# Query/key projection and gate/up: the token halves in the innermost loop of the matmuls

## The chip, the core and the metric

The kernel runs on one core of a Trainium2 chip. The metric is the device time of one execution in microseconds. The engines have these names in all rows: PE is TensorE's matmul, PEld its weight load (it runs beside PE), DVE is VectorE, ACT ScalarE, POOL GpSimd, SP SyncE, which issues the DMAs. Each engine works off its own instructions in order and waits for the others through semaphores.

## What is computed

A trunk of two layers over 1024 tokens of 1024 features in float32. The first layer mixes tokens by differential attention (8 heads, two softmax maps each), the second by neighbourhood attention (16 heads on a 16 x 64 grid). Around them stand norms, residual sums, a gated FFN with 2816 hidden units, and a gated input per layer:

```python
def swiglu(h, w_gate, w_up, w_down):
    return (jax.nn.silu(h @ w_gate) * (h @ w_up)) @ w_down
...
    for i in range(DEPTH):
        hn = rmsnorm(h, norm_mix[i])
        ...
            mix = diff_attention(hn, da_w_qkv[j], da_w_o[j], ...)
        ...
            mix = neighborhood_attention(hn, na_w_qkv[j], na_b_qkv[j], na_rpb[j], na_w_o[j])
        h = h + mix
        h = h + swiglu(rmsnorm(h, norm_ffn[i]), ffn_w_gate[i], ffn_w_up[i], ffn_w_down[i])
        gate = jax.nn.sigmoid(rmsnorm(h, norm_ple[i]) @ ple_w_gate[i])
        h = h + gate * (p[i] @ ple_w_proj[i])
    return rmsnorm(h, norm_final)
```

## The kernel before

**Products.** Every float32 matrix is held as two float32r parts, high and low (`split`, L87: one engine copies the high part, VectorE subtracts it from the source to get the low part). A product is three matmuls, high x high, high x low, low x high (`PASSES`, L49: stationary part, moving part). Line L131 (`mm_feat`) makes products whose result has features on the partitions: a weight tile of 128 x 128 is stationary, and a token half of 512 columns is moving. It is used for the query and key projections of both attentions (`qk`, L143) and for gate and up of the FFN (`hidden`, L532). Line L139 (`mm_tok`) makes products with tokens on the partitions (the down projection and out_proj): its innermost loop already runs over two halves of the columns, into two accumulators. L209 makes the values, L495 and L139 the two parts of out_proj, L595 and L599 the gated input.

**Operands.** The normalised tokens lie transposed in `hnT[0]` (tokens 0 to 511, token tiles 0 to 3) and `hnT[1]` (512 to 1023, tiles 4 to 7), in a pool on the right side of SBUF. In the orders of instructions below they are called hnT_95 and hnT_96 (layer 0, attention), hnT_6900 and hnT_6901 (layer 0, FFN), hnT_17330 and hnT_17331 (layer 1, FFN). `weights` (L94) loads 512 KB on SP's queue into a stage tile, GpSimd copies the high part into a slab on the left side (L91), VectorE writes the low part (L92). The pool in which out_proj_first keeps its operands (L495) takes the place of hnT while hnT is closed.

**Norm.** `norm_t` (L117) takes token tile t: ScalarE squares and sums (L111), GpSimd makes the factor (L112, L113), VectorE scales (L114), PE transposes eight 128 x 128 blocks (L124) into two PSUM tiles, ScalarE copies their high part into hnT (L89) and VectorE the low part (L92). At the end of out_proj each tile is first added to its residual by VectorE (L518).

**FFN.** For each of 22 hidden blocks of 128, gate and then up get an accumulator of 1024 columns (two PSUM banks, three such accumulators in all), then Silu on ScalarE reads the whole gate accumulator and VectorE multiplies by the whole of up. After every second block the down projection adds two blocks into the residual (L550).

**Attention.** The projections' accumulators of 512 columns come from a pool of two ("d"; four during the first projection). ScalarE reads an accumulator out into the high part (L162 to L166), VectorE into the low part (L170, L173), GpSimd copies the key to the other half of the partitions (L185).

**Order.** The program is written tile by tile, and a list scheduler decides, per engine, in which order the instructions are issued; a matmul whose accumulator isn't free, or whose operands aren't ready, can be passed by others when that order is made, but not when the program runs.

Of the kernel before, what the change touches and what calls it, by code (L numbers as in the profile page):

```python
# [12 lines left out]
F32 = mybir.dt.float32  # L13
# [7 lines left out]
P = 128  # L21
# [20 lines left out]
MASKED = -1e30  # L42
RING = 5
EARLY = 5
# heads whose two maps are scored together, so that their 64-row products share the array
PAIRED = 4
EXP_LN_SET = 6
# the three products that carry a float32 product: (stationary part, moving part)
PASSES = ((0, 0), (0, 1), (1, 0))  # L49


class Trunk:
# [21 lines left out]
        self.hs = self.dram.tile([NT, P, D], F32, name="hs")  # L74
        self.hp = self.dram.tile([NT, P, D], F32, name="hp")

# [1 line left out]
    def open_hn(self):  # L78
        self.hnpool = self.tc.alloc_tile_pool(name=self.nc.get_next_instruction_name(), bufs=1, side="right",
                                              reuse_waits="tile")  # L80
# [44 lines left out]
            ks = slice(4 * q, 4 * q + 4)  # L125
            self.split((dst[:, 0, ks, c], dst[:, 1, ks, c]), tr, self.nc.scalar)

    def mm_feat(self, ps, w, half):
        for kt in range(KT):
            for n, (i, j) in enumerate(PASSES):  # L130
                self.nc.tensor.matmul(ps, w[:, i, kt * P:(kt + 1) * P], self.hnT[half][:, j, kt, :],  # L131
                                      start=kt == 0 and n == 0, stop=kt == KT - 1 and n == 2)

    def mm_tok(self, ps, lhs, rhs, nk):
        for k in range(nk):
# [3 lines left out]
                    self.nc.tensor.matmul(ps[:, c], lhs(i, k), rhs(j, k, c),  # L139
                                          start=k == 0 and n == 0, stop=k == nk - 1 and n == 2)  # L140

# [1 line left out]
    def qk(self, u, pools, bias=None, q_scale=1.0):  # L143
        nc = self.nc
        qkp, psd = pools["qk"], pools["d"]
        qs = qkp.tile([P, 2, S], F32R, tag=f"qs{u % 2}", name="qs")
        kh = qkp.tile([P, 2, S], F32R, tag=f"kh{u % 2}", name="kh")
        kl = qkp.tile([P, S], F32R, tag=f"kl{u % 2}", name="kl")
        top, bot = slice(0, 64), slice(64, 128)
        for which in range(2):  # L150
            w = self.weights(pools["wqk"][2 * u + which], self.slab, "slab")
            b = None if bias is None else bias[:, which * 8 + u:which * 8 + u + 1]
            for half in range(2):
                c = slice(half * HALF, (half + 1) * HALF)
                ps = psd.tile([P, HALF], F32, tag="d", name="d")
                self.mm_feat(ps, w, half)

                sc = q_scale if which == 0 else 1.0

                def hi(out, rows):  # L160
                    if b is None and sc == 1.0:
                        nc.scalar.copy(out=out, in_=ps[rows])  # L162
                    elif b is None:
                        nc.scalar.activation(out=out, in_=ps[rows], func=AF.Copy, scale=sc)
                    else:
                        nc.scalar.activation(out=out, in_=ps[rows], func=AF.Identity, bias=b[rows], scale=1.0)  # L166

                def lo(out, rows, h):
                    if b is None:
                        nc.vector.scalar_tensor_tensor(out=out, in0=ps[rows], scalar=sc, in1=h.bitcast(F32),  # L170
                                                       op0=ALU.mult, op1=ALU.subtract)
                    else:
                        nc.vector.scalar_tensor_tensor(out=out, in0=ps[rows], scalar=b[rows], in1=h.bitcast(F32),  # L173
                                                       op0=ALU.add, op1=ALU.subtract)

                if which == 0:
                    hi(qs[top, 0, c], top)
                    hi(qs[bot, 1, c], bot)
                    lo(qs[bot, 0, c], top, qs[top, 0, c])
                    lo(qs[top, 1, c], bot, qs[bot, 1, c])  # L180
                else:
                    hi(kh[top, 0, c], top)
                    hi(kh[bot, 1, c], bot)
                    for m, (to, src) in enumerate(((bot, top), (top, bot))):
                        nc.gpsimd.tensor_scalar(out=kh[to, m, c], in0=kh[src, m, c].bitcast(F32), scalar1=1.0,  # L185
                                                scalar2=0.0, op0=ALU.mult, op1=ALU.add)
                    lo(kl[top, c], top, kh[top, 0, c])
                    lo(kl[bot, c], bot, kh[bot, 1, c])
        return qs, kh, kl
# [21 lines left out]
                                          start=k == 0 and n == 0, stop=k == KT - 1 and n == 2)  # L211
            sink(t, ps)

# [1 line left out]
    def diff_attention(self, first):  # L215
        nc, tc, a = self.nc, self.tc, self.a
        with ExitStack() as st:
# [133 lines left out]
                    ops = project(h + 1)  # L351
            self.out_proj_first(0, a["da_wo"], psd)

# [1 line left out]
    def neighborhood_attention(self):  # L355
        nc, tc, a = self.nc, self.tc, self.a
        with ExitStack() as st:
# [103 lines left out]
                    ops = self.qk(u + 1, pools, bq)  # L461
            self.out_proj_first(1, a["na_wo"], psd)

# [1 line left out]
    def keep(self, layer, u, ot):  # L465
        if u == PAIRS - 1:
            self.last = ot
# [54 lines left out]
    def ffn(self, layer, h, ps):  # L522
        nc, tc, a = self.nc, self.tc, self.a
        starts = [0] + list(range(1, NHID - 2, 2))
        with ExitStack() as st:
            actp = st.enter_context(tc.tile_pool(name=f"act{layer}", bufs=1, reuse_waits="tile"))
            wdp = st.enter_context(tc.tile_pool(name=f"wd{layer}", bufs=1, reuse_waits="tile"))
            gp = st.enter_context(tc.tile_pool(name=f"gf{layer}", bufs=1, reuse_waits="tile"))
            g = self.gain(3 * layer + 2, gp)
            acts, wds = {}, {}  # L530

            def hidden(n):  # L532
                pss = []
                for which in range(2):
                    w = self.weights(a["gu"][layer, n, which], self.slab, "slab")
                    acc = ps.tile([P, S], F32, tag="mm", name="mm")
                    for half in range(2):
                        self.mm_feat(acc[:, half * HALF:(half + 1) * HALF], w, half)
                    pss.append(acc)
                sil = self.t4.tile([P, S], F32, tag="t4", name="sil")  # L540
                nc.scalar.activation(out=sil, in_=pss[0], func=AF.Silu)  # L541
                nc.vector.tensor_tensor(out=sil, in0=sil, in1=pss[1], op=ALU.mult)  # L542
                acts[n] = actp.tile([P, 2, S], F32R, tag=f"act{n % 4}", name="act")
                self.split((acts[n][:, 0], acts[n][:, 1]), sil, nc.scalar)
                wds[n] = self.weights(a["wd"][layer, n * P:(n + 1) * P], wdp, f"wd{n % 3}")

            def down(c0, step):
                for t in range(NT):
                    acc = ps.tile([P, D], F32, tag="mm", name="mm")
                    self.mm_tok(acc, lambda i, k: acts[c0 + k][:, i, t * P:(t + 1) * P],  # L550
                                lambda j, k, c: wds[c0 + k][:, j, c], step)
                    nc.vector.tensor_tensor(out=h[t], in0=h[t], in1=acc, op=ALU.add)  # L552
                    if c0 + step >= NHID:
                        self.norm_t(h[t], t, g)

            for n in range(NHID):
                hidden(n)
                if n in starts[1:]:
                    c0 = starts[starts.index(n) - 1]
                    down(c0, n - c0)  # L560
            down(starts[-1], NHID - starts[-1])
# [77 lines left out]
        self.close_hn()  # L639


# [1 line left out]
def _units(w, n, width):  # L643
    k = w.shape[0]
    return w.reshape(k // P, P, n, width).transpose(2, 1, 0, 3)
# [64 lines left out]
```

## Time and profile before

| | us |
|---|---|
| median of 3 runs | 3075.58 |
| lowest and highest run | 3072.76, 3077.97 |
| span of the profiled execution | 3072.8 |
| PE busy in it | 3025.0 |
| VectorE, ScalarE, GpSimd busy | 1524.7, 783.0, 625.2 |

The profiled execution is the lowest of the three runs: its time, 3072.76 us, is its span. The stages follow one another: the first norm and projections (to 60 us), the attention of layer 0 (to 743), its out_proj and norm (to 803), its FFN (to 1525), the gated input (to 1648), the same for layer 1. Matmuls are pipelined: the duration of one, from its start to the modelled end, is longer than the distance to the next, so the busy time of PE is no measure of how fast it works.

### The profile page before, as it was taken

What the parts mean: (1) busy time and instruction counts of PE and PEld (TensorE: products, weight loads), DVE (VectorE), ACT (ScalarE), POOL (GpSimd) and SP (SyncE); (2) the same over time, 40 slices, a digit from 0 to 9 for tenths busy, and PEclk for the clock granted to TensorE, in tenths of its full rate; (3) what the DMA queues carried; (4) which work ended last, traced back from release to release, by engine and by line L of the source; (5) the groups of instructions that cost most, each with busy time, mean ns of one, the idle gap of its engine ahead of it and who ended that gap; (6) DMA issues with size and microseconds to landing.
All of it is one profiled execution on the core that took longest, in us unless ns stands there. A gap on an engine that the chain in (4) does not pass through costs nothing.

```text
span 3072.8 us, 36422 instructions
## 1 busy us (share of the span) xinstructions
PE 3025.0 (98%) x14304; PEld 2410.6 (78%) x14304; DVE 1524.7 (50%) x2793; ACT 783.0 (25%) x1576; POOL 625.2 (20%) x766
## 2 busy tenths in 40 slices
PE   7999999999999999999999999999999999999998
PEld 7777777677788888888888878877778888888886
DVE  5677777775622323333444565666533333322354
ACT  3445454443200000000212444543200000000021
POOL 2232333332200000010112332332210001000121
PEclk9999999999999999999999999999999999999999
DMA  3010101243211111111123121136321111111112
GB/s 132 15 42 28 42 28 35 73 147 113 94 48 48 49 48 48 42 48 54 38 74 102 39 82 54 60 104 203 129 62 48 42 48 49 48 48 49 50 45 78
DMA packets 83866, 198.54 MB, mean 65 GB/s; under 512 B 6768, under 2 KB 39664, under 8 KB 83696
## 3 DMA queue, kind: packets, MB, share of 16 engines
q1 hardware_dynamic: 83696, 196.22, 20.4%
q8 instruction: 113, 1.85, 0.3%
q14 instruction: 57, 0.47, 0.1%
HBM read 164.74 MB, written 31.46 MB: 64 GB/s over the span
## 4 chain that ended last, share of the span: by engine, by line
PE 96%; DVE 2%; DMA 1%; issue 1%; ACT 0%; POOL 0%; POOLq 0%; SPq 0%; DVEq 0%; ACTq 0%
PE mm L131 32%; PE mm L139 17%; PE d L131 12%; PE d L209 7%; PE mm L599 6%; PE s L196 5%; PE d L495 3%; PE av L312 3%; PE s L193 3%; PE tr L306 2%; PE mm L595 1%; PE o L407 1%; PE tr L124 1%; PE tr L432 1%; DMA st<-da_wo 0%
## 5 line engine op out<-in xcount | busy, mean ns | idle before, releaser
L131 PE MATMUL mm<-hnT,w 128*128 128x512 f32 x4224 | 997.9, 397 | 2.5 <-DVE h L518 1.5
L131 PEld LDWEIGHTS mm<-hnT,w 128*128 128x128 f32 x4224 | 796.1, 189 | 197.5 <-POOL rs L113 1.7
L91 POOL TENSOR_SCALAR w<-st 128x1024 fp32r<-128x1024 f32 (+1 forms) x248 | 256.1, 1034 | 1619.2 <-PE mm L131 794.4
L92 DVE TENSOR_TENSOR w<-st,w 128x1024 fp32r<-128x1024 f32 (+1 forms) x248 | 282.8, 1142 | 490.1 <-POOL w L91 489.7
L139 PE MATMUL mm<-w,act 128*128 128x512 f32 x2112 | 486.0, 390 | 0.9 <-DVE h L552 0.9
L139 PEld LDWEIGHTS mm<-w,act 128*128 128x128 f32 x2112 | 395.7, 188 | 83.9 <-DVE h L552 1.7
L131 PE MATMUL d<-hnT,w 128*128 128x512 f32 x1536 | 405.0, 407 | 0.0
L131 PEld LDWEIGHTS d<-hnT,w 128*128 128x128 f32 x1536 | 280.1, 189 | 80.6 <-issue 22.2
L552 DVE TENSOR_TENSOR h<-h,mm 128x1024 f32<-128x1024 f32 x176 | 213.6, 1218 | 153.6 <-PE mm L139 153.2
L541 ACT ACTIVATE sil<-mm 128x1024 f32<-128x1024 f32 x44 | 45.4, 1031 | 791.4 <-PE mm L131 791.4
L542 DVE TENSOR_TENSOR sil<-sil,mm 128x1024 f32<-128x1024 f32 x44 | 53.7, 1221 | 374.1 <-PE mm L131 374.1
L209 PE MATMUL d<-w,hnT 128*128 128x256 f32 x1536 | 236.4, 295 | 1.6 <-POOL w L91 1.1
L209 PEld LDWEIGHTS d<-w,hnT 128*128 128x128 f32 x1536 | 201.2, 191 | 26.2 <-issue 21.8
L92 DVE TENSOR_TENSOR at<-tr,at 128x512 fp32r<-128x512 f32 (+2 forms) x288 | 157.4, 552 | 69.3 <-ACT at L89 56.0
L599 PE MATMUL mm<-w,hnT 128*128 128x512 f32 x768 | 188.4, 397 | 0.0
L281 ACT ACTIVATE e<-e,mx 128x1024 f32<-128x1024 f32 x128 | 147.2, 1150 | 130.9 <-DVE mx L279 126.1
L89 ACT CAST at<-tr 128x512 fp32r<-128x512 f32 (+2 forms) x288 | 133.6, 483 | 167.6 <-PE tr L432 106.2
L196 PE MATMUL s<-kl,qs 64*128 64x512 f32 (+2 forms) x384 | 175.5, 473 | 0.0
L89 ACT CAST act<-sil 128x1024 fp32r<-128x1024 f32 x44 | 46.4, 1054 | 489.6 <-DVE sil L542 489.6
L599 PEld LDWEIGHTS mm<-w,hnT 128*128 128x128 f32 x768 | 143.1, 188 | 33.5
L193 PE MATMUL s<-kh,qs 128*128 128x512 f32 (+2 forms) x384 | 156.7, 414 | 7.3 <-DVE kl L170 3.1
L196 PEld LDWEIGHTS s<-kl,qs 64*128 64x128 f32 x384 | 68.2, 183 | 93.5 <-issue 91.0
(101 smaller groups left out, 3003.0 us busy)
## 6 DMA issues: line engine op xcount, KB each, us to landing
st<-gu SPq DMA_DIRECT2D x88, 512.0 KB, 3.6
st<-wd SPq DMA_DIRECT2D x44, 512.0 KB, 3.5
ot<-ot SPq DMA_DIRECT2D x28, 512.0 KB, 3.9
o<-ot SPq DMA_DIRECT2D x16, 640.0 KB, 4.7
st<-da_qk SPq DMA_DIRECT2D x16, 512.0 KB, 3.6
hp<-r SPq DMA_DIRECT2D x16, 512.0 KB, 4.7
r<-hp SPq DMA_DIRECT2D x16, 512.0 KB, 3.5
st<-wpg SPq DMA_DIRECT2D x16, 512.0 KB, 3.6
```

Of the source, the lines that this page charges most:

```text
L89: hi_engine.copy(out=w[0], in_=src)
L91: hi_engine.tensor_scalar(out=w[0], in0=src, scalar1=1.0, scalar2=0.0, op0=ALU.mult, op1=ALU.add)
L92: self.nc.vector.tensor_tensor(out=w[1], in0=src, in1=w[0].bitcast(F32), op=ALU.subtract)
L131: self.nc.tensor.matmul(ps, w[:, i, kt * P:(kt + 1) * P], self.hnT[half][:, j, kt, :], start=kt == 0 and n == 0, stop=kt == KT - 1 and n == 2)
L139: self.nc.tensor.matmul(ps[:, c], lhs(i, k), rhs(j, k, c), start=k == 0 and n == 0, stop=k == nk - 1 and n == 2)
L193: self.nc.tensor.matmul(s, qs[:, m, qc], kh[:, m, kc], start=True, stop=False)
L196: self.nc.tensor.matmul(s, qs[b, m, qc], kl[b, kc], start=False, stop=True)
L209: self.nc.tensor.matmul(ps, self.hnT[t // 4][:, i, k, c], ws[k // 4][:, j, (k % 4) * 256:(k % 4 + 1) * 256], start=k == 0 and n == 0, stop ...
L281: nc.scalar.activation(out=e[m], in_=e[m], func=AF.Exp, bias=mx[:, m:m + 1], scale=SLOPES[h], accum_out=sm[:, m:m + 1])
L312: nc.tensor.matmul(av, v[:, kb, x], at[:, y, kb, :], start=kb == 0 and n == 0, stop=kb == NT - 1 and n == 2)
L552: nc.vector.tensor_tensor(out=h[t], in0=h[t], in1=acc, op=ALU.add)
L599: nc.tensor.matmul(acc[:, 0], self.hnT[t // 4][:, i, k, cs], ws[k // 2][:, j, k % 2], start=k == 0 and n == 0, stop=k == KT - 1 and n == 2)
```

## The change

`mm_feat` gets both accumulators. For each of the eight blocks of the contraction and each of the three passes it issues the matmul for token half 0 and then that for half 1, with the same stationary tile. In `qk` both "d" tiles are taken before the products and read out after them, one after the other; in `hidden` the two halves of the 1024-column accumulator are handed over together. The number of matmuls, the tiles and their places stay the same. (The diff also drops comments; they are left out here.)

```diff
-    def mm_feat(self, ps, w, half):
+    def mm_feat(self, ps, w):
         for kt in range(KT):
             for n, (i, j) in enumerate(PASSES):
-                self.nc.tensor.matmul(ps, w[:, i, kt * P:(kt + 1) * P], self.hnT[half][:, j, kt, :],
-                                      start=kt == 0 and n == 0, stop=kt == KT - 1 and n == 2)
+                for half in range(2):
+                    self.nc.tensor.matmul(ps[half], w[:, i, kt * P:(kt + 1) * P], self.hnT[half][:, j, kt, :],
+                                          start=kt == 0 and n == 0, stop=kt == KT - 1 and n == 2)
...
             b = None if bias is None else bias[:, which * 8 + u:which * 8 + u + 1]
+            pss = [psd.tile([P, HALF], F32, tag="d", name="d") for _ in range(2)]
+            self.mm_feat(pss, w)
             for half in range(2):
                 c = slice(half * HALF, (half + 1) * HALF)
-                ps = psd.tile([P, HALF], F32, tag="d", name="d")
-                self.mm_feat(ps, w, half)
-
+                ps = pss[half]
...
                     acc = ps.tile([P, S], F32, tag="mm", name="mm")
-                    for half in range(2):
-                        self.mm_feat(acc[:, half * HALF:(half + 1) * HALF], w, half)
+                    self.mm_feat([acc[:, half * HALF:(half + 1) * HALF] for half in range(2)], w)
```

In the changed program the lines behind L131 have moved by one (L131 is L132, L139 is L140, L193 and L196 are L194 and L197, L312 is L313). What the scheduler makes of it is shown at three places.

PE where layer 0 goes from out_proj to the FFN, the difference of the two orders (minus: before, plus: changed). The transposes are those of token tiles 4 to 7:

```order
 L124 MATMUL tr<-ident,n 128x128 x8
-L131 MATMUL mm<-hnT_6900,w 128x512 x24
+L132 MATMUL mm<-hnT_6900,w 128x512
 L124 MATMUL tr<-ident,n 128x128 x8
-L131 MATMUL mm<-hnT_6900,w 128x512 x24
+L132 MATMUL mm<-hnT_6900,w 128x512
 L124 MATMUL tr<-ident,n 128x128 x8
-L131 MATMUL mm<-hnT_6900,w 128x512 x24
+L132 MATMUL mm<-hnT_6900,w 128x512
 L124 MATMUL tr<-ident,n 128x128 x8
-L131 MATMUL mm<-hnT_6901,w 128x512 x72
```

Three bursts of 24 matmuls on half 0 stood between the transposes; one matmul of each burst stays there, and the other 23 come behind the last transposes.

PE at the same place of layer 1, before:

```order
L124 MATMUL tr<-ident,n 128x128 x8
L131 MATMUL mm<-hnT_17330,w 128x512 x2
L124 MATMUL tr<-ident,n 128x128 x4
L131 MATMUL mm<-hnT_17330,w 128x512 x19
L124 MATMUL tr<-ident,n 128x128 x4
L131 MATMUL mm<-hnT_17330,w 128x512 x22
L124 MATMUL tr<-ident,n 128x128 x8
L131 MATMUL mm<-hnT_17330,w 128x512 x24
L124 MATMUL tr<-ident,n 128x128 x8
L131 MATMUL mm<-hnT_17330,w 128x512 x5
L124 MATMUL tr<-ident,n 128x128 x8
L131 MATMUL mm<-hnT_17331,w 128x512 x72
```

and changed:

```order
L124 MATMUL tr<-ident,n 128x128 x8
L132 MATMUL mm<-hnT_17330,w 128x512 x2
L124 MATMUL tr<-ident,n 128x128 x8
L132 MATMUL mm<-hnT_17330,w 128x512
L124 MATMUL tr<-ident,n 128x128 x24
L132 MATMUL mm<-hnT_17331,w 128x512
L132 MATMUL mm<-hnT_17330,w 128x512
L132 MATMUL mm<-hnT_17331,w 128x512
```

Here, too, three of 72 matmuls are left between the transposes, and behind them the halves alternate, as they do in the rest of both FFNs.

PE in the attention of layer 0, in the query projection of the third head, before:

```order
L131 MATMUL d<-hnT_95,w 128x512 x4
L193 MATMUL s<-kh,qs 128x512
L196 MATMUL s<-kl,qs 128x512
L131 MATMUL d<-hnT_96,w 128x512 x13
L312 MATMUL av<-at,v 128x256
L131 MATMUL d<-hnT_96,w 128x512
```

and changed:

```order
L194 MATMUL s<-kh,qs 128x512
L197 MATMUL s<-kl,qs 128x512
L132 MATMUL d<-hnT_95,w 128x512 x2
L132 MATMUL d<-hnT_96,w 128x512 x9
L313 MATMUL av<-at,v 128x256
L132 MATMUL d<-hnT_96,w 128x512
```

Here the half 0 of this projection still runs to its end before half 1 begins; the two differ only in where the scores stand between them.

## Rows read from the trace of the kernel before

**Rows 1.** The page: busy time by engine, and the chain by engine.

```profile
PE 3025.0 (98%) x14304; PEld 2410.6 (78%) x14304; DVE 1524.7 (50%) x2793; ACT 783.0 (25%) x1576; POOL 625.2 (20%) x766
...
PE 96%; DVE 2%; DMA 1%; issue 1%; ACT 0%; POOL 0%; POOLq 0%; SPq 0%; DVEq 0%; ACTq 0%
```

**Rows 2.** Windows: stretch, length, busy per engine (matmuls), granted clock, DMA share, GB/s.

```profile
60.00:743.00 683.00, 671.35 (x3391) 498.40 (x3389) 501.68 (x1206) 323.00 (x651) 224.18 (x247) 0.99 0.18 55
...
803.00:1525.00 722.00, 721.22 (x3128) 585.21 (x3126) 248.67 (x212) 59.16 (x68) 75.03 (x80) 1.00 0.16 48
...
1696.00:2160.00 464.00, 458.11 (x2413) 365.97 (x2413) 283.00 (x842) 208.50 (x544) 143.03 (x198) 1.00 0.29 93
```

**Rows 3.** The page's groups: line, engine, operation, count, busy us, mean ns, idle before.

```profile
L131 PE MATMUL mm<-hnT,w 128*128 128x512 f32 x4224 | 997.9, 397 | 2.5 <-DVE h L518 1.5
...
L139 PE MATMUL mm<-w,act 128*128 128x512 f32 x2112 | 486.0, 390 | 0.9 <-DVE h L552 0.9
L139 PEld LDWEIGHTS mm<-w,act 128*128 128x128 f32 x2112 | 395.7, 188 | 83.9 <-DVE h L552 1.7
L131 PE MATMUL d<-hnT,w 128*128 128x512 f32 x1536 | 405.0, 407 | 0.0
```

**Rows 4.** Timeline of PE, four stretches of one line: start, length, line, count.

```profile
1243.00 45.14 PE L131 MATMUL mm<-hnT,w 128*128 128x512 f32 x192
1287.97 21.93 PE L139 MATMUL mm<-w,act 128*128 128x512 f32 x96
...
1566.21 5.77 PE L599 MATMUL mm<-w,hnT 128*128 128x512 f32 x24
...
2109.64 2.88 PE L495 MATMUL d<-w,o 128*128 128x512 f32 x12
```

**Rows 5.** Timeline of PE at the entry of layer 0's FFN.

```profile
783.08 5.42 PE L131 MATMUL mm<-hnT,w 128*128 128x512 f32 x22 [0.33 <-DVE w L92]
...
801.32 1.03 PE L124 MATMUL tr<-ident,n 128*128 128x128 f32 x8
802.60 28.39 PE L131 MATMUL mm<-hnT,w 128*128 128x512 f32 x120 [0.24 <-ACT hnT L89]
```

**Rows 6.** Timeline there: the adds of tiles 4, 5, 7, the scaling of 7.

```profile
775.23 1.22 DVE L518 TENSOR_TENSOR h<-mm,r 128x1024 f32<-128x1024 f32 x1
...
780.69 1.21 DVE L518 TENSOR_TENSOR h<-mm,r 128x1024 f32<-128x1024 f32 x1
...
793.87 1.21 DVE L518 TENSOR_TENSOR h<-mm,r 128x1024 f32<-128x1024 f32 x1
...
798.00 1.28 DVE L114 SCALAR_TENSOR_TENSOR n<-h,rs,g 128x1024 f32<-128x1024 f32 x1
```

**Rows 7.** Timeline at the entry of layer 1's FFN, several engines.

```profile
2201.28 6.67 PE L131 MATMUL mm<-hnT,w 128*128 128x512 f32 x19
...
2205.74 1.21 DVE L518 TENSOR_TENSOR h<-mm,r 128x1024 f32<-128x1024 f32 x1
...
2208.42 0.59 ACT L89 CAST hnT<-tr 128x512 fp32r<-128x512 f32 x1 [6.17 <-PE tr L124]
...
2212.53 1.28 DVE L114 SCALAR_TENSOR_TENSOR n<-h,rs,g 128x1024 f32<-128x1024 f32 x1 [0.72 <-POOL rs L113]
...
2223.19 28.39 PE L131 MATMUL mm<-hnT,w 128*128 128x512 f32 x120
```

**Rows 8.** Windows at that entry, columns as in rows 2.

```profile
2196.00:2199.00 3.00, 1.21 (x8) 0.72 (x5) 2.69 (x3) 1.32 (x3) 2.05 (x3) 0.97 0.54 179
...
2202.00:2205.00 3.00, 3.00 (x9) 2.32 (x8) 2.56 (x3) 0.25 (x1) 1.62 (x2) 0.50 0.62 217
```

**Rows 9.** Timeline at the first scores: key copies, key subtractions, scores of half 1.

```profile
71.39 1.18 ACT L162 CAST kh<-d 64x512 fp32r<-64x512 f32 x2 [4.44 <-PE d L131]
...
73.84 1.39 DVE L170 SCALAR_TENSOR_TENSOR kl<-d,kh 64x512 fp32r<-64x512 f32 x2
...
75.37 0.47 PE L193 MATMUL s<-kh,qs 128*128 128x512 f32 x1 [3.14 <-DVE kl L170]
```

## The prediction

> **What bounds the kernel now.** I first read the page. TensorE (PE) is busy for 98% of the span, and the chain of work that ended last lies on PE for 96% of it [rows 1]. The table by stages says the same stage by stage: in the FFN of layer 0 PE is busy 721.2 of 722 us, in the first attention 671.4 of 683, in the second 458.1 of 464, and no other engine comes near it [rows 2]. So what counts is how closely matmuls follow each other, and where PE has nothing to run.
>
> Next came the groups. L131, the line that the change rewrites, has 4224 matmuls in the FFNs and 1536 in the attentions. All lines together have 14304 matmuls and 14304 weight loads [rows 1], of 188 ns each on L139 [rows 3]. A "busy" matmul overlaps the next one (397 ns each on average, far above their spacing), so I took the spacing from stretches of PE's timeline that hold one line only: length less one duration, divided by the number less one. That gives (45.14 - 0.40) / 191 = 234.2 ns for L131 and (21.93 - 0.39) / 95 = 226.7 ns for L139 [rows 4]. A load of 188 ns ends within the 227 to 234 ns of the matmul before it; it isn't what sets the spacing.
>
> **The change, part by part.** *Weight loads.* L139 already does what L131 is to do: one stationary tile, half 0, half 1, two accumulators. It still has 2112 loads for 2112 matmuls [rows 3]. So I count 5760 loads before and after, each behind a matmul: 0 us.
>
> In the Trainium skill, "TensorE: Matmul & The Clock Gate", step 1 of "What happens when you issue a matmul" says that weights can be loaded once and used for many matmuls. By this 2880 of the 5760 loads would go, and if the loads were what held the matmuls up, the sum would fall by what rival A gives. The rows on L139 speak against it: the same tile twice in succession, and a load each time.
>
> *Spacing of the matmuls.* This is where the change could gain: 7.5 ns for each of 5760 matmuls would be 43 us. Is L139 faster because of its loop order? Two other lines answer. L495 has L131's old order (high, high, low stationary part, one accumulator at a time, up to 15 products each) and yet settles at (2.88 - 0.39) / 11 = 226.4 ns; L599 has the old order too, and takes (5.77 - 0.40) / 23 = 233.5 [rows 4]. So the order doesn't separate fast from slow. What does is the operands: L131 and L599 read hnT against a weight tile from a pool on the left side of SBUF; L139 and L495 read two operands of one side. In the program hnT starts at a byte address 32 past a multiple of 64, the left pools at a multiple of 64; both operands of L495 are 32 past, both of L139 at a multiple. The changed program has the same addresses. I therefore take 234 ns before and after: 0 us, with a gain of 31 us in the FFNs as the other end.
>
> *The attentions.* There the order of instructions shows that the scheduler undoes most of the change: two "d" accumulators are all there are, and half 0 still runs through before half 1. In 8 of 32 projections both halves now end together, so that both accumulators are read out and released at once. Other work stands between them in the queue, as it did before. PE's idle time in both attentions is 11.7 + 5.9 us [rows 2], which bounds a gain from a luckier order; I take 0, and -8 to +8 for the range. For the first projection the 96 matmuls take as long as before, but the key's half 0 is no longer read out while half 1 runs. The first scores, at 71.2 us, now wait for ScalarE's two copies (1.18 us together [rows 9]) and the rest of the key path; before, the scores of half 1 waited for the same path, 3.14 us [rows 9]. So the wait moves forward more than it grows: +1 us (0 to 3).
>
> *Entering an FFN.* Here the change costs. Before, the first 72 matmuls of gate and up need hnT of half 0 only (tokens of tiles 0 to 3), and stand in the queue as bursts of 2 + 22, 24 and 24 between the transposes of tiles 4 to 7. They cover the norm of the last four tiles ([rows 5] has the first 22; the other bursts are alike). Now the second matmul of each weight tile needs half 1, so one matmul is left between the transposes, three in all, and 69 have to come after the last norm: 69 x 0.2342 = 16.2 us of work that loses its cover. From this goes what PE gets back by restarting sooner.
>
> Layer 0. The restart was at 802.60 us. The normalised tile 7 was ready at 798.00 + 1.28 = 799.28, and its transposes started at 801.32: they stood 2.0 us behind a burst [rows 5, 6]. Without bursts they start at 799.3 and the restart is at about 800.4. At best the adds of tiles 6 and 7 follow at the pace that held before, 780.69 - 775.23 = 5.46 us, tile 7's at 791.6; with the chain of 799.28 - 793.87 = 5.4 us and 1.3 for transposes and copy [rows 5, 6] that is 798.3. At worst nothing comes sooner. Loss: 16.2 - 2.2 = **14.0 us** (11.9 to 16.2).
>
> Layer 1. The restart was at 2223.19 us, yet tile 7 was ready at 2212.53 + 1.28 = 2213.8; its transposes stood behind bursts. Its norm was late as well: ScalarE's copy waited 6.17 us for a transpose queued behind a burst of 19 that took 6.67 us, and the square of tile 7 stood behind that copy [rows 7]. From the add at 2205.74, 5.4 us of chain and 1.3 give 2212.4; the add itself stood behind such work too, so I take 2211 (2207 to 2215). Loss: 16.2 - 12.2 = **4.0 us** (0 to 8.0).
>
> *The clock.* In layer 1 PE was busy for only 1.21 of the 3 us from 2196 on, and its granted clock then went to 0.50 (1.2 GHz instead of 2.4) [rows 8]; the burst of 19 took 6.67 us instead of 19 x 0.234 = 4.45, 2.2 us more [rows 7]. With about 18 us of near-idle at both entries I expect that price once at each restart: **+4.4 us** (0 to 6.8).
>
> The Trainium skill (same page, "Why this matters for your kernels") warns of idle gaps between bursts of matmuls that throw the clock back; the stretch above agrees. It is a rule against this change: without it the sum would be 4.4 us less.
>
> The rest of the FFN is unchanged: Silu and the product read whole accumulators of 1024 columns, so a half that used to finish early served nobody.
>
> **Sum.** 14.0 + 4.0 + 4.4 + 1 = +23.4 us, against the profiled execution's 3072.8 us: 3096.2. The median of the runs is 2.8 us above that execution, so I give 3075.6 + 23.4 = **3099 us**. All low ends with 8 us of attention off: 3080; all high ends: 3118.
>
> **The rivals.** *A: L131 goes to L139's spacing*, as the loop order would have it if the bank change between neighbouring matmuls mattered. Some 4190 neighbours in the FFNs and 207 in the attentions now alternate: 4397 x 7.5 ns = 33 us off, 3066 us. It turns the sign once the spacing falls by more than 23.4 us / 4397 = 5.3 ns, to 228.9. For it: L139. Against: L495. *B: both accumulators released together stall PE.* This ends on the slower side, beyond my forecast: in 8 projections the next d tile waits for two pairs of ScalarE copies and VectorE subtractions, 2 x (1.2 + 1.4) us [rows 9]; if the queue holds half as much ready work, 8 x 2.6 = 21 us would come on top at most, about 10 as I see it: 3109. It decides as soon as the work queued behind the pair is shorter than 5.2 us. *C: the entries cost little*, because the norms, no longer queued behind bursts, run at 3 us a tile instead of 5.46, and the attentions gain a little: +2 us, 3078. Against it stands the pace of 5.46 us, measured where PE wasn't the last to be waited for.
>
> **Chances and range.** Forecast 0.64 (3085 to 3108 by itself), A 0.10, B 0.16, C 0.10. A measurement of this kernel tells about 0.2%, 6 us, from no change. The forecast and B are slower by more than that; C is within it; A is mostly faster, a small part of it within: faster 0.09, same 0.11, slower 0.80. The range leaves out A, half of C and the top of B: 3078 to 3113.
>
> **What would show it.** Right: single-line stretches of L132 at 234 ns, as many weight loads as matmuls, PE idle for some 14 us between out_proj's last matmul and the FFN's start in either layer, restart near 800 and 13 us after tile 4's transposes in layer 1, a clock of 0.50 there, stages of the attentions as long as before within 8 us. Wrong: a spacing near 227 (A), fewer loads than matmuls, more idle time of PE behind ScalarE and VectorE in the attentions (B), or entries that last no longer than before (C).

## The result, and the profile after

The changed kernel takes 3109.0 us, the kernel before 3075.7 (medians of four runs each): a ratio of 1.0111, 95% interval 1.0096 to 1.0125, or 33.4 us more. The forecast was 3099 us, slower, with a range of 3078 to 3113. The sign and the range hold; the size is 10 us short, and the runs below say where.

The page of the changed kernel, with the rows that answer [rows 1] and [rows 3] (L131 is now L132, L139 is L140, L193 is L194):

```profile
PE 3036.4 (98%) x14304; PEld 2418.1 (78%) x14304; DVE 1526.0 (49%) x2793; ACT 780.5 (25%) x1576; POOL 627.8 (20%) x766
...
PE 93%; DVE 2%; DMA 1%; issue 1%; ACT 1%; POOL 1%; POOLq 0%; SPq 0%; DVEq 0%; ACTq 0%
...
L132 PE MATMUL mm<-hnT,w 128*128 128x512 f32 x4224 | 998.3, 398 | 5.4 <-POOL w L91 2.9
L132 PEld LDWEIGHTS mm<-hnT,w 128*128 128x128 f32 x4224 | 797.7, 189 | 200.6 <-POOL w L91 3.6
...
L132 PE MATMUL d<-hnT,w 128*128 128x512 f32 x1536 | 402.6, 407 | 0.0
```

There are as many weight loads as before, one for each matmul, though two neighbours now use the same weight tile. TensorE's share of the chain falls from 96 to 93%. The stretch of the FFN that answers the first of [rows 4], in the timeline of PE (start, length, line, count), has the same length to the hundredth:

```profile
1261.96 45.14 PE L132 MATMUL mm<-hnT,w 128*128 128x512 f32 x192
```

That is (45.14 - 0.40) / 191 = 234.2 ns, as before. So the steady state didn't move, and the loss lies at the ends of stages. Here is where, in us, from the starts of instructions in the profiled executions: the first scores; from there to out_proj's first matmul of L139; from there to the 73rd matmul of gate/up; from there to the first matmul of L599; and the same for layer 1, whose attention is counted from its first score.

| stage | before | changed | difference |
|---|---|---|---|
| to the first scores | 71.2 | 73.1 | +1.9 |
| rest of attention, layer 0 | 672.6 | 673.9 | +1.3 |
| entry of the FFN, layer 0 | 58.8 | 74.8 | +15.9 |
| FFN to its end, layer 0 | 725.6 | 725.5 | -0.1 |
| attention, layer 1 | 465.0 | 469.5 | +4.6 |
| entry of the FFN, layer 1 | 63.2 | 73.7 | +10.5 |
| FFN to its end, layer 1 | 725.6 | 725.5 | -0.2 |

PE at the entry of layer 0, which answers [rows 5] (the releaser of a wait stands in brackets):

```profile
785.26 0.47 PE L132 MATMUL mm<-hnT,w 128*128 128x512 f32 x1
789.92 1.94 PE L124 MATMUL tr<-ident,n 128*128 128x128 f32 x8 [4.18 <-DVE n L114]
791.51 0.78 PE L132 MATMUL mm<-hnT,w 128*128 128x512 f32 x1
797.24 1.94 PE L124 MATMUL tr<-ident,n 128*128 128x128 f32 x8 [4.96 <-DVE n L114]
798.84 0.78 PE L132 MATMUL mm<-hnT,w 128*128 128x512 f32 x1
803.03 1.94 PE L124 MATMUL tr<-ident,n 128*128 128x128 f32 x8 [3.42 <-DVE n L114]
804.79 21.54 PE L132 MATMUL mm<-hnT,w 128*128 128x512 f32 x88
```

Where bursts of 22 to 24 matmuls stood, one matmul is left, and PE waits 4.18, 4.96 and 3.42 us for the next normalised tile. The waits are what the bursts used to cover. The windows of both entries, columns as in [rows 2]: layer 0 from the first single matmul to the restart, then the 69 that came behind it; the same for layer 1.

```profile
785.26:804.79 19.53, 6.96 (x27) 5.50 (x27) 15.52 (x17) 6.44 (x13) 7.79 (x9) 0.60 0.51 161
804.79:821.70 16.91, 16.91 (x70) 13.62 (x70) 2.59 (x3) 2.90 (x3) 1.05 (x1) 0.96 0.04 7
...
2220.40:2239.30 18.90, 9.53 (x35) 6.99 (x36) 16.85 (x18) 6.77 (x12) 6.07 (x8) 0.56 0.48 141
2239.30:2257.40 18.10, 18.10 (x72) 14.50 (x71) 1.92 (x2) 2.90 (x3) 1.05 (x1) 0.89 0.11 31
```

PE is idle for 12.6 us in the first window of layer 0 and 9.4 us in that of layer 1 (some 14 in either were forecast). In layer 1 VectorE (the third engine column) is busy for 16.85 of the 18.9 us.

### The profile page after: what moved, and what is told of

Same layout as the page of the kernel before. It is cut to its first block, busy times and chain, and to the rows that moved or that the text cites. A ratio compares the mean times of both kernels' runs of the same rounds, so it can differ in the third digit from the quotient of the medians.

```text
span 3106.8 us, 36425 instructions
## 1 busy us (share of the span) xinstructions
PE 3036.4 (98%) x14304; PEld 2418.1 (78%) x14304; DVE 1526.0 (49%) x2793; ACT 780.5 (25%) x1576; POOL 627.8 (20%) x766
## 4 chain that ended last, share of the span: by engine, by line
PE 93%; DVE 2%; DMA 1%; issue 1%; ACT 1%; POOL 1%; POOLq 0%; SPq 0%; DVEq 0%; ACTq 0%
PE mm L132 32%; PE mm L140 16%; PE d L132 12%; PE d L210 7%; PE mm L599 6%; PE s L197 4%; PE d L496 4%; PE av L313 3%; PE s L194 3%; PE tr L307 2%; PE mm L595 1%; PE o L408 1%; PE tr L433 1%; PE tr L124 1%; DVE w L92 1%
## 5 line engine op out<-in xcount | busy, mean ns | idle before, releaser
L132 PE MATMUL mm<-hnT,w 128*128 128x512 f32 x4224 | 998.3, 398 | 5.4 <-POOL w L91 2.9
L132 PEld LDWEIGHTS mm<-hnT,w 128*128 128x128 f32 x4224 | 797.7, 189 | 200.6 <-POOL w L91 3.6
L140 PE MATMUL mm<-w,act 128*128 128x512 f32 x2112 | 485.9, 390 | 0.9 <-DVE h L552 0.9
L140 PEld LDWEIGHTS mm<-w,act 128*128 128x128 f32 x2112 | 395.6, 188 | 83.9 <-DVE h L552 1.7
L132 PE MATMUL d<-hnT,w 128*128 128x512 f32 x1536 | 402.6, 407 | 0.0
L132 PEld LDWEIGHTS d<-hnT,w 128*128 128x128 f32 x1536 | 281.3, 189 | 80.2 <-issue 21.1
L599 PE MATMUL mm<-w,hnT 128*128 128x512 f32 x768 | 188.5, 397 | 0.0
L197 PE MATMUL s<-kl,qs 64*128 64x512 f32 (+2 forms) x384 | 175.6, 474 | 0.0
L599 PEld LDWEIGHTS mm<-w,hnT 128*128 128x128 f32 x768 | 143.1, 188 | 33.6
L194 PE MATMUL s<-kh,qs 128*128 128x512 f32 (+2 forms) x384 | 159.0, 419 | 5.5 <-POOL kh L186 2.1
L197 PEld LDWEIGHTS s<-kl,qs 64*128 64x128 f32 x384 | 68.2, 184 | 92.6 <-issue 89.7
```

The lines of the kernel that those rows point to most:

```text
L132: self.nc.tensor.matmul(ps[half], w[:, i, kt * P:(kt + 1) * P], self.hnT[half][:, j, kt, :], start=kt == 0 and n == 0, stop=kt == KT - 1 a ...
L140: self.nc.tensor.matmul(ps[:, c], lhs(i, k), rhs(j, k, c), start=k == 0 and n == 0, stop=k == nk - 1 and n == 2)
L194: self.nc.tensor.matmul(s, qs[:, m, qc], kh[:, m, kc], start=True, stop=False)
L197: self.nc.tensor.matmul(s, qs[b, m, qc], kl[b, kc], start=False, stop=True)
L599: nc.tensor.matmul(acc[:, 0], self.hnT[t // 4][:, i, k, cs], ws[k // 2][:, j, k % 2], start=k == 0 and n == 0, stop=k == KT - 1 and n == 2)
```

## The experiments

### The two halves of the change, each alone

The first kernel has the new order in gate and up only, the second in the query/key projection only.

```diff
-                    self.mm_feat([acc[:, half * HALF:(half + 1) * HALF] for half in range(2)], w)
+                    for half in range(2):
+                        self.mm_feat_old(acc[:, half * HALF:(half + 1) * HALF], w, half)
```

(this is the edit of the second kernel to the changed one; the first has the like in `qk`)

> The new order in gate and up alone; the query/key projection as before. Theory (the entries): the trace of the changed kernel puts 15.8 us of its loss at the entry of layer 0's FFN and 10.5 us at that of layer 1, so 3075.7 + 26.3 = 3102 us, with both attentions as long as before (683.8 us from 60 us to out_proj and 454.8 from layer 1's first transpose of the weights to out_proj, both within 1 us), and L131's successor at 234 ns. Rival (the attentions' loss comes from elsewhere than the projection's order, for instance from what the queues hold ahead of the FFN): they lose their 3 and 5 us here too, 3110 us.

> The new order in the query/key projection alone; gate and up as before. Theory: the 3.2 us of the first attention and 4.7 of the second belong to this part, 3075.7 + 7.9 = 3084 us, with PE's idle time in the two attentions up by some 4 us (1.9 of it before the first scores) and the entries as before (restart of gate/up 58.8 and 63.2 us after out_proj's start). Rival (they come from the FFN's part): 3076 us.

Gate and up alone: 3104.0 us against 3075.4, ratio 1.0094 (1.0078 to 1.0109), +28.6 us. The entries take 74.7 and 73.1 us from out_proj's start, nearly as in the changed kernel. The projection alone: 3082.8 us, ratio 1.0022 (1.0012 to 1.0032), +7.4 us; the entries are 58.8 and 63.2 us, as before, and the first scores come at 73.0. So four fifths of the loss belong to gate and up. One expectation failed: with the old projection in the first kernel, each attention still took 2.5 us longer than in the trace of before (675.1 and 467.5 us). Over all kernels with hnT at its old address the attention of layer 1 takes 463.8 to 467.6 us with the old projection, and 468.0 to 470.3 with the new one: longer by some 3 us, in a scatter of nearly the same size.

### The first two hidden blocks in the old order

```diff
-                    self.mm_feat([acc[:, half * HALF:(half + 1) * HALF] for half in range(2)], w)
+                    if n < 2:
+                        for half in range(2):
+                            self.mm_feat_old(acc[:, half * HALF:(half + 1) * HALF], w, half)
+                    else:
+                        self.mm_feat([acc[:, half * HALF:(half + 1) * HALF] for half in range(2)], w)
```

> The changed kernel with the first two hidden blocks of each FFN in the old order (half 0 through, then half 1), the other 20 in the new one. If the whole loss in the FFNs is the cover lost at their entry, 26.3 us come back: 3109 - 26.3 = 3083 us, and the same 72 matmuls of half 0 as before stand between the transposes. If the alternation of the halves costs something in every block (rival), no more than 2/22 of that part comes back, and the time stays above 3095.

3083.5 us, ratio 1.0027 (1.0017 to 1.0037): 25.5 us of the 33.4 are back, with 20 of 22 blocks in the new order. PE at the entry of layer 0 in this kernel has its bursts again (L138 holds the old loop; a third burst of 24 follows):

```profile
785.52 0.70 PE L138 MATMUL mm<-hnT,w 128*128 128x512 f32 x2
786.56 5.42 PE L138 MATMUL mm<-hnT,w 128*128 128x512 f32 x22 [0.34 <-DVE w L92]
791.82 1.03 PE L124 MATMUL tr<-ident,n 128*128 128x128 f32 x8
792.61 5.87 PE L138 MATMUL mm<-hnT,w 128*128 128x512 f32 x24
```

So the loss in the FFNs is, within a microsecond, the cover of the norms: the two entries take 59.4 and 63.2 us again, and from the 73rd matmul to their end both FFNs take 725.6 us, as before. Alternating the halves costs nothing in the other blocks, and brings nothing.

### What sets the spacing: 32 bytes

The prediction rested on a claim that no trace had shown: L131 is slower than L139 because of where its operands lie, not because of its loops. First the rule as the prediction had it, multiples of 64 bytes, on the kernel before:

```diff
+        pad = tc.alloc_tile_pool(name="pad", bufs=1, side="right")
+        self.pad = pad.tile([P, 8], F32, name="pad")
+        nc.vector.memset(self.pad, 0.0)
         self.open_hn()
```

> The kernel before, with 32 bytes per partition set aside at the right end of SBUF, so that both hnT tiles start at a multiple of 64 bytes instead of 32 past one; loop orders and instructions as before. Theory (the place of the operands sets the spacing, not the loop order): L131 falls from 234.2 to 226.7 ns with its old order, and L599 from 233.5 to 226.7: 5760 x 7.5 + 768 x 6.8 = 43 + 5 = 48 us off, 3028 us. Rival (L139 is faster for its loop order, two accumulators in turn): L131 and L599 stay at 234 ns, 3076 us.

3066.6 us, ratio 0.9974 (0.9962 to 0.9985): 9 us off, not 48. The stretch of 192 matmuls takes 44.95 us:

```profile
1241.03 44.95 PE L131 MATMUL mm<-hnT,w 128*128 128x512 f32 x192
```

That is 233.2 ns. A small move of an address does change the spacing, so the loop order isn't all there is, but the rule was wrong. The four lines of [rows 4] also differ, in the program's allocation, in the distance from the stationary tile to the moving row, modulo 512 bytes: it is 0 in L139 and in L495, 160 in L131 and 352 in L599; the 32 bytes made it 128 for L131.

### A scan of the distance, in both loop orders

```diff
+            for order in range(2):
+                for d in range(16):
+                    ...
+                    for kt, n, half in steps:
+                        i, j = PASSES[n]
+                        o = j * KT * HALF + kt * HALF + 8 * d
+                        nc.tensor.matmul(acc[:, half], w[:, i, kt * P:(kt + 1) * P], flat[half][:, o:o + HALF],
+                                         start=kt == 0 and n == 0, stop=kt == 6 and n == 2)
```

> The kernel before with 32 groups of 42 matmuls put in ahead of the first attention: weights and hnT as in the query/key projection (7 of 8 k tiles, three products each), the moving rows shifted by 0, 32, ... 480 bytes; 16 groups with half 0 through and then half 1, 16 with the halves in turn. Their sums are read out and thrown away. It adds some 1344 x 0.23 = 310 us; only the spacing in the groups is read. Theory that the first alignment run left (what counts is the distance of the moving row from the weights' address, modulo 512 bytes; it is 160 in L131, 0 in L139 and in L495): 234 ns at shift 0, 227 where the shift brings the distance to 0 or 512 (shift 352), values between elsewhere, and the same in both orders. Rival 1 (both operands on one side of SBUF, wherever they lie): 234 in all 32 groups but for the slow ones. Rival 2 (loop order): the 16 groups in turn some 7 ns below the 16 others.

The mean spacing inside each group from its third matmul on, in the one execution of this kernel, by the distance modulo 256 bytes from the weights to the moving rows (the first two groups, which still had other work among them, are left out):

| distance, bytes | 0 | 32 | 64 | 96 | 128 | 160 | 192 | 224 |
|---|---|---|---|---|---|---|---|---|
| half 0, then half 1 (ns) | 227.0 | 233.4 | 228.9 | 233.6 | 233.4 | 234.1 | 233.3 | 233.2 |
| halves in turn (ns) | 227.0 | 233.4 | 228.9 | 233.6 | 233.4 | 234.1 | 233.3 | 233.2 |

Where two groups of an order have the same distance modulo 256, they agree within 0.1 ns. Windows of four groups, columns as in [rows 2], each from its first matmul to that of the next group: halves in turn at the distances 192 and 0, then half 0 first at 0 and 64.

```profile
197.89:207.68 9.79, 9.79 (x43) 7.86 (x42) 0.00 (x0) 1.02 (x1) 0.00 (x0) 1.00 0.13 54
217.48:227.02 9.54, 9.54 (x43) 7.88 (x42) 0.00 (x0) 1.01 (x1) 0.00 (x0) 1.00 0.13 55
61.48:71.02 9.54, 9.54 (x43) 7.88 (x42) 0.00 (x0) 1.02 (x1) 0.00 (x0) 1.00 0.14 57
80.83:90.44 9.61, 9.61 (x43) 7.89 (x42) 0.00 (x0) 1.02 (x1) 0.00 (x0) 1.00 0.13 55
```

42 matmuls start in each: 9.54 / 42 = 227 ns, 9.61 / 42 = 229, 9.79 / 42 = 233. In all four the clock is at 1.00 (2.4 GHz). Both rivals fall: the operands lie on two sides of SBUF in every group, and the two orders give the same numbers. The distance counts modulo 256 bytes, not 512.

The scan moves only the moving rows, so by itself it can't tell their distance from their address. [Rows 4] can: the moving rows of L495 start at 480 modulo 512 bytes in the program's allocation, as those of L131 do, yet L495 ran at 226.4 ns and L131 at 234.2; and the stationary tiles of L131 and of L139 both start at 320, at 234.2 and 226.7 ns. Neither address decides alone.

### The same in the kernel: 160 bytes

The edit is the one above with a tile of 40 instead of 8 floats.

> The kernel before with 160 bytes per partition set aside at the right end of SBUF, so that hnT has the weight tiles' address modulo 512 (320) and the out-projection's early part keeps both its operands alike. Theory (distance modulo 512): L131 and L599 at 227 ns with the old loop order, 5760 x 7.4 + 768 x 6.8 = 43 + 5 = 48 us off, 3028 us. Rival (side of SBUF): 234 ns, 3066 to 3076 us.

3031.1 us against 3076.8, ratio 0.9852 (0.9837 to 0.9866): faster than both kernels of the case, with the old loops. Timeline of PE, in the FFN and in L599's stage:

```profile
1228.37 43.68 PE L131 MATMUL mm<-hnT,w 128*128 128x512 f32 x192
1271.89 21.92 PE L139 MATMUL mm<-w,act 128*128 128x512 f32 x96
...
1544.94 5.60 PE L599 MATMUL mm<-w,hnT 128*128 128x512 f32 x24
```

(43.68 - 0.40) / 191 = 226.6 ns for L131 and (5.60 - 0.40) / 23 = 226.1 for L599. In L131 hnT is the moving operand and in L599 the stationary one, so the padding shifted the moving rows of one line and the stationary tiles of the other; both lines fell.

### The aligned kernel with the change

> The changed kernel with the 160 bytes set aside, so that all operands of L132 lie alike modulo 256. Theory (the new loop order has no part in the spacing, its cost at the entries and in the first scores is the same): L132 at 227 ns, the same 33 us above the aligned kernel in the old order: 3031 + 33 = 3064 us. Rival (once the operands lie alike, turns of two banks or two uses of one weight tile bring something more): spacing under 226 ns, 5760 x 1 ns = 6 us off or more, 3058 us or less.

3062.8 us, ratio to before 0.9959 (0.9945 to 0.9973): 31.8 us above the aligned kernel in the old order, at the same spacing:

```profile
1254.75 37.56 PE L132 MATMUL mm<-hnT,w 128*128 128x512 f32 x165
```

(37.56 - 0.40) / 164 = 226.6 ns. Within the noise of the two ratios, the change costs the same with the operands alike.

### The reverse edit in L139

```diff
-        for k in range(nk):
-            for n, (i, j) in enumerate(PASSES):
-                for half in range(2):
-                    c = slice(half * HALF, (half + 1) * HALF)
+        for half in range(2):
+            c = slice(half * HALF, (half + 1) * HALF)
+            for k in range(nk):
+                for n, (i, j) in enumerate(PASSES):
```

> The kernel before with the reverse edit in L139 (the down projection and the late part of out_proj): half 0 through all products, then half 1, one accumulator bank at a time, a new stationary tile for nearly each matmul. Theory (where the operands lie): L139 stays at 227 ns, 3076 us but for a few us at the stages' ends. Rival (loop order makes L139 faster): 234 ns, 2400 x 7.4 = 18 us more, 3094 us.

3090.1 us, ratio 1.0044 (1.0029 to 1.0059). By the time alone the rival would be the nearer one. The timeline decides:

```profile
1226.32 21.93 PE L139 MATMUL mm<-w,act 128*128 128x512 f32 x96
```

This is the length of [rows 4], 226.7 ns, in the other loop order. (A new stationary tile comes for two of each three matmuls there, as the first two passes share one.) The time went to the ends of stages: 6.2 us at the entry of layer 0, and 3.5 and 3.3 us in the rest of the two FFNs, of which all but 0.4 us comes behind the last matmul of gate and up. I didn't follow the cause.

### What holds up the restart in layer 1

The restart came 55.7 us after out_proj's start, 63.2 before the change; the forecast had about 51. In the trace of the changed kernel, PE at that entry:

```profile
2220.43 0.47 PE L132 MATMUL mm<-hnT,w 128*128 128x512 f32 x1 [0.33 <-ACT hnT L89]
2222.97 0.77 PE L132 MATMUL mm<-hnT,w 128*128 128x512 f32 x1 [2.07 <-DVE h L519]
2225.32 1.97 PE L124 MATMUL tr<-ident,n 128*128 128x128 f32 x8 [1.59 <-DVE hnT L92]
2230.21 0.80 PE L132 MATMUL mm<-hnT,w 128*128 128x512 f32 x1 [2.92 <-POOL w L91]
2230.80 1.91 PE L124 MATMUL tr<-ident,n 128*128 128x128 f32 x8
2234.31 1.97 PE L124 MATMUL tr<-ident,n 128*128 128x128 f32 x8 [1.60 <-DVE hnT L92]
2236.82 1.12 PE L124 MATMUL tr<-ident,n 128*128 128x128 f32 x4 [0.55 <-DVE hnT L92]
2238.56 1.12 PE L124 MATMUL tr<-ident,n 128*128 128x128 f32 x4 [0.62 <-DVE hnT L92]
2239.33 22.87 PE L132 MATMUL mm<-hnT,w 128*128 128x512 f32 x89
```

My first theory was that the single matmuls stop the transposes behind them. With half 1 first in the first two blocks, no such matmul is left there:

```diff
-                for half in range(2):
+                for half in halves:
...
+                                 (1, 0) if n < 2 else (0, 1))
```

> The changed kernel with half 1 ahead of half 0 in the innermost loop of the first two hidden blocks of each FFN: then no matmul of gate and up stands between the transposes of the last four tiles, and all 72 follow them. Theory (in layer 1 the three single matmuls left between the transposes held these up: they waited 2.07 us for an accumulator and 2.92 us for the split of a weight tile, and tile 5, normalised at 2221.7, was transposed at 2230.8): layer 1 restarts 3 to 4 us sooner, three more matmuls cost 0.7 us in each layer, 3109 - 2.5 = 3106.5 us. Rival (VectorE's queue and the chain of each norm set the end, the single matmuls stop nobody): no restart moves, 3109 + 1.4 = 3110.4 us.

3111.3 us, ratio 1.0111 (1.0094 to 1.0128). The rival is right: layer 1 restarts 55.7 us after out_proj's start, as it did. PE's waits between 2215 and 2245 us of this kernel (line, releaser, us in total, times, longest) all name the same releaser:

```profile
PE tr L124 <- DVE hnT L92: 11.5, 5, 5.3
```

A transpose needs one of two PSUM tiles; the one before is free when VectorE has subtracted from it, and in VectorE's queue the splits of weight tiles, and the adds and scalings of later token tiles, stand ahead of that. The timeline of VectorE in the changed kernel, columns as for PE:

```profile
2222.74 1.92 DVE L92 TENSOR_TENSOR w<-st,w 128x1024 fp32r<-128x1024 f32 x1
2224.59 1.27 DVE L92 TENSOR_TENSOR hnT<-tr,hnT 128x512 fp32r<-128x512 f32 x2
2225.78 1.21 DVE L92 TENSOR_TENSOR w<-st,w 128x1024 fp32r<-128x1024 f32 x1
2226.92 1.27 DVE L114 SCALAR_TENSOR_TENSOR n<-h,rs,g 128x1024 f32<-128x1024 f32 x1
2228.11 1.21 DVE L519 TENSOR_TENSOR h<-mm,r 128x1024 f32<-128x1024 f32 x1
...
2232.37 1.28 DVE L114 SCALAR_TENSOR_TENSOR n<-h,rs,g 128x1024 f32<-128x1024 f32 x1 [0.72 <-POOL rs L113]
2233.57 1.28 DVE L92 TENSOR_TENSOR hnT<-tr,hnT 128x512 fp32r<-128x512 f32 x2
2236.08 0.69 DVE L92 TENSOR_TENSOR hnT<-tr,hnT 128x512 fp32r<-128x512 f32 x1 [1.23 <-ACT hnT L89]
```

So the next kernel takes those splits away from VectorE:

```diff
+        if no_low:
+            self.nc.scalar.activation(out=w[1], in_=src, func=AF.Copy, scale=0.0)
+        else:
+            self.nc.vector.tensor_tensor(out=w[1], in0=src, in1=w[0].bitcast(F32), op=ALU.subtract)
```

> The changed kernel, but the low parts of the weights of the first two hidden blocks of each FFN (gate, up and down) are not the difference that VectorE takes, but zeros written by ScalarE, so that some low products of these blocks are left out of the result (not of the work of TensorE). It takes about five subtractions of 1.2 us from VectorE's queue in the entry of layer 1, where VectorE was busy for 16.85 of 18.9 us between the first and the fourth matmul of gate and up. Theory (VectorE's queue sets the restart there: the transposes wait for its subtractions on hnT, and these stand behind the splits of weights): from out_proj's start to the 73rd matmul layer 1 takes 68 to 71 us instead of 73.7; layer 0, where nothing is queued, 73 to 75 instead of 74.75; 3105 us. Rival (the chain of each norm and the two PSUM tiles of the transposes at 1.2 GHz set it): 73.7 as before, 3109 us.

3105.7 us, ratio 1.0101 (1.0086 to 1.0116), 3.4 us under the changed kernel; the intervals of the two ratios overlap, so the entries have to decide. That of layer 1 takes 71.0 instead of 73.7 us, that of layer 0 74.1 instead of 74.8. The entry of layer 1 also took 73.1 and 72.9 us in two other kernels with the changed order (gate and up alone, and the aligned kernel), so the edit gave 2 to 2.7 us there, at the lower end of what the theory allowed. The end of tile 7's norm, on GpSimd and VectorE, and the restart of PE in this kernel:

```profile
2229.97 1.04 POOL L91 TENSOR_SCALAR w<-st 128x1024 fp32r<-128x1024 f32 x1 [1.64 <-DMA st<-wd]
2230.98 0.55 POOL L116 TENSOR_TENSOR rs<-ms,mhalf 128x1 f32<-128x1 f32 x1
2231.56 1.28 DVE L117 SCALAR_TENSOR_TENSOR n<-h,rs,g 128x1024 f32<-128x1024 f32 x1 [2.83 <-POOL rs L116]
```

```profile
2236.78 9.59 PE L135 MATMUL mm<-hnT,w 128*128 128x512 f32 x35
```

From tile 7's normalisation to the restart it still takes 2236.78 - 2232.84 = 3.9 us, where the changed kernel took 2239.33 - 2233.65 = 5.7. But a new wait came in: GpSimd's factor for tile 7 stands in its queue behind the copy of a weight tile that waits for its load, and VectorE, which waits 2.83 us for that factor, has the next subtraction on hnT behind it. From its add at 2225.13 tile 7's norm took 7.7 us, 5.5 in the changed kernel. So 2 to 2.7 us is what this edit gave, not all that the splits cost. What is left fits the rival in part: two PSUM tiles, and transposes at half the clock, 1.97 us for eight instead of 1.03. The other part is GpSimd's queue, and no run separates the two.

## Why the prediction was right, and where it was short

- **Weight loads, 0 us: right.** 14304 before and after, and the same spacing. The Trainium skill's step 1 of "What happens when you issue a matmul" ("TensorE: Matmul & The Clock Gate"), by which weights can be loaded once and used for many matmuls, did not come into play here, as the rows on L139 had said.
- **Spacing, 0 us: right in its result, by a rule that was wrong.** The argument that the loop order doesn't separate fast from slow lines, drawn from L495 and L599, holds: 20 blocks in the new order cost nothing, the reverse edit left L139 at 226.7 ns, and the scan gives the same figures in both orders. That the operands' place does it holds too. But the place is the distance of moving rows and weights modulo 256 bytes, not a multiple of 64: with the address at a multiple of 64 L131 took 233.2 ns. The addresses are the same in the changed kernel, so the wrong rule gave the right 0. Rival A falls with it. The prediction also took from a load's 188 ns that loads don't set the spacing; this is not settled, for the address of the tile that is loaded has a part in it.
- **Entry of layer 0, +14.0 and 2.2 for the clock: 15.9 measured.** 69 matmuls (16.2 us) lost their cover, the restart came 1.0 us sooner (57.8 instead of 58.8 us after out_proj's start; 2.2 were forecast), and the 69 took 16.91 instead of 16.2, 0.7 for the clock. The transposes of tile 7 did start as soon as it was normalised, as forecast; but its norm took 5.9 us from the add (797.01 to 802.88) instead of 5.4, and transposes and copy 1.8 (803.03 to 804.79) instead of 1.3, as the eight transposes took 1.94 us instead of 1.03.
- **Entry of layer 1, +4.0 and 2.2: 10.5 measured.** This step failed in size: without the clock it is 16.2 - 7.5 = 8.7 us, outside the stated 0 to 8.0. I let the restart follow tile 7's add by 5.4 us of chain and 1.3 for transposes and copy. The chain took 2233.65 - 2228.11 = 5.5, but the last part 5.7: the transposes had piled up behind VectorE and two PSUM tiles. The trace of before didn't show this; there the bursts stood between the transposes. So the restart came 7.5 us sooner, not 12.2. The clock's part was 18.10 - 16.2 = 1.9 us.
- **The clock, +4.4: 2.6 measured.** The granted clock fell in the idle stretches, to 0.60 and 0.56 in their windows (layers 0 and 1), and stood at 0.96 and 0.89 in the windows of the 69 matmuls behind, where 1.00 is 2.4 GHz and 0.50 is 1.2. The rule of the skill that I weighed (same page, "Why this matters for your kernels": no idle gaps between bursts) is borne out in kind, at less than the price of [rows 7].
- **First scores, +1: 1.9 measured**, inside the stated 0 to 3. The wait is the rest of the key path, GpSimd's copies of the high part first and then, for half 1, VectorE's subtraction:

```profile
73.06 0.50 PE L194 MATMUL s<-kh,qs 128*128 128x512 f32 x1 [1.88 <-POOL kh L186]
...
76.42 0.76 PE L194 MATMUL s<-kh,qs 128*128 128x512 f32 x1 [1.73 <-DVE kl L171]
```

- **The attentions, 0: 5.9 measured**, 1.3 and 4.6, inside the stated 8. Some three of the 4.6 belong to the projection by the runs above, the rest can't be told from the scatter. Rival B, whose time (3109) the result happens to hit, is not the reason: a projection's matmuls wait for a d tile for 0.0 us in the page above. The wait that grew is that of the attention's own products in layer 1 (line, releaser, us in total, times, longest; the first row is of before, the others of the changed kernel):

```profile
PE o L407 <- ACT at L89: 2.0, 2, 1.8
```

```profile
PE o L408 <- ACT at L89: 3.8, 4, 1.3
PE o L408 <- DVE at L92: 1.2, 1, 1.2
PE o L408 <- ACT kh L167: 0.9, 1, 0.9
```

The last row names the readout of a key: in the new order both halves of a key are copied together, and the copies stand ahead of the attention's own in ScalarE's queue. The waits of these products (L407 before, L408 changed) come to 6.1 or 6.2 us in all six kernels with the new projection, and to 1.8 or 2.0 in all six with the old one. Other waits shrank, so that PE's idle time in layer 1's attention is 7.3 to 8.2 us with the new projection and 4.9 to 6.7 with the old: some 2 us. The rest is time in which PE was busy, and that varies by some 3 us among kernels with the same projection. That ScalarE's queue is the reason was not tested.

Summed up, the entries were forecast 4 us too short and the attentions with the first scores 7: together 11 us in the profiled executions, for the 10 us by which the forecast missed the medians. The range held with some luck. 3109.0 us lies just beyond the 3085 to 3108 that the forecast gave itself; the top of the range was there for rival B, which didn't happen.

## What to carry to other kernels

Before the order of a loop is changed, look at what its first turns cover: an outer loop over halves may be there, in effect, to start on the half that is ready, and the first two blocks of 22 were worth 25.5 of 33.4 us. When two lines with the same matmul differ by a few per cent, compare the addresses of their operands before the order of their loops; here 160 bytes of padding gave 46 us, more than any order. And where work that covered a chain is taken away, sum up each engine's work in the gap anew: a queue that was never late can become the one that is waited for.

## What was not expected of the hardware

A stream of 128x512 float32r matmuls with a weight load each ran at 227.0 ns a matmul where the moving rows and the weight tile start at the same address modulo 256 bytes, at 228.9 where the moving rows start 64 bytes past the weight tile, and at 233.2 to 234.1 at the six other distances that the scan tried, in both loop orders, at the full clock. Matmuls of 256 columns showed no such gain: in L209 the median spacing was 120 ns before and 120 with the operands alike.

The Trainium skill ("TensorE: Matmul & The Clock Gate", "What happens when you issue a matmul", step 1) says that weights are loaded through a read port of their own, so that a load doesn't steal bandwidth from the running matmul. The scan doesn't show which part of the engine or of SBUF makes the distance matter; it shows that the addresses of the two streams aren't without effect on each other. No run here takes the loads away, so whether the loads are what the moving rows collide with stays open.
